# Where a row block of 640 keys is divided in the pass for row maxima and sums: 384 and 256 in place of 512 and 128

## The chip, the core and the metric

The kernel runs on one core of a Trainium2 chip. TensorE (PE in the rows) multiplies, VectorE (DVE), ScalarE (ACT) and GpSimd (POOL) do the elementwise work, and SyncE (SP) issues nearly all transfers. The metric is the device time of one execution in microseconds (us); lower is better.

## What is computed

One layer of a hybrid decoder on 1024 positions of 1024 channels: norm, one input projection, four head groups (A: sparse attention in three branches, B: differential attention, C: retention, D: a state space scan), gates, one output projection, residual, norm. The change touches only the softmax statistics of groups A and B. Cut to that:

```python
# group B, per head and map: all keys up to the query
s = einsum(q, k) * scale - slope * (t_q - t_k)
p = masked_softmax(s, t_q >= t_k)             # exp(s - max) / sum

# group A, branch "slc": as above (all 16 blocks of 64 keys are chosen)
# group A, branch "win": only the last 512 positions
p_w = masked_softmax(s_w, (dist >= 0) & (dist < WINDOW))
```

## The kernel before, in words

Positions are 8 blocks of 128, in two halves `u` of four blocks. Each attention head is worked twice. A **row pass** (`diff_rows` for group B, `nsa_rows` for A) has queries on partitions and only finds, for each query, the maximum and the sum of exponentials; `Stats.tile` does that for one tile of scores in PSUM. A second pass (`diff_out`, `nsa_out`) has keys on partitions, takes the shifts that the row pass left, and multiplies by the values into a bank `O`.

In the row pass a block `i` of 128 queries sees `n = (i + 1) * 128` keys, or at most 640 in the branch "win" (block `i` and the four before it). A bank of PSUM holds 512 float32 columns, so the keys are walked in pieces of 512. One piece is: matmul into a bank `S` (L173; in `nsa_rows` a second one at L1015 or L1026 for the low parts and positions), then `Stats.tile`: on VectorE the maximum (L466 without a mask, L468 with one), then on ScalarE the exponential with its sum (L469). The bank is free after that. There are three `S` banks, shared with the second pass. A matmul always takes at least 256 key columns, of which the statistics may use fewer, so that a last piece of 128 keys is multiplied as 256. A piece of at most 256 keys shares its bank: in `diff_rows` with the same piece of the other map, in `nsa_rows` (for `i % 4 < 2`) with the piece of the other branch.

A block of exactly 640 keys occurs in block 4 of both maps of four heads of group B, in block 4 of "slc" and in blocks 4 to 7 of "win" of four heads of group A: 28 blocks of 640 keys in all.

The order on each engine is made when the program is built: three streams (attention, recurrent groups, projections with the output at their end) are interleaved by weights, projection matmuls are kept behind a score matmul of some banks before, and a scheduler then orders the instructions of each engine by its own idea of their durations. So a change of one instruction's size can move others. GpSimd takes the low parts of weights (L248, L1182: raw minus high part) and parts of the second pass (L1083, L1085); SyncE's queue carries the loads and stores in order.

At the end `out_final` multiplies positions by the last two k tiles of the output weights (L1192 to L1194) into banks `mm` and `R`, and closes with the norm; the last steps of `nsa_out` (L1090) run among its first ones.

Of the kernel before, what the change touches and what calls it, by code (L numbers as in the profile page):

```python
# [20 lines left out]
S = 1024  # L21
D = 1024
# [32 lines left out]
def shape_constants():  # L55
    """Arrays that depend on the shapes alone: masks, decays, position rows."""
# [36 lines left out]
def merge(*streams):  # L93
    """Interleaves (generator, steps) streams in proportion to their steps; one that yields False waits for others."""
# [29 lines left out]
def hybrid_trunk_kernel(ctx: ExitStack, tc: tile.TileContext, a, out, dbg=None):  # L124
# [46 lines left out]
    def scores(tile_, *args, **kw):  # L171
        """A matmul into a bank of scores; the first of each bank paces the projections."""
        ins = T.matmul(tile_, *args, **kw)  # L173
        if kw["start"]:
            pace.append(ins)

    def paced(ins):
        """Keeps a projection's matmul behind the scores of a few banks before."""
        if len(pace) > AHEAD + FREE:
            tc.add_manual_dep(ins.ins, pace[-1 - AHEAD].ins.name, NOSYNC, reason="pace")  # L180

    def bc(ap, n):
        """[P, a] -> [P, a, n], each value repeated."""
        return ap[:, :, None].to_broadcast([ap.shape[0], ap.shape[1], n])

# [36 lines left out]
    def rsqrt_mean(dst, ssq, n):  # L222
        """dst = (ssq / n + eps) ** -0.5 on small tiles."""
# [10 lines left out]
    def weights(w, cols):  # L234
        """hi and lo parts of the columns `cols` = [(offset, width), ...] of w, by k tile."""
# [16 lines left out]
    def proj_t(cols, evac):  # L252
        """Columns on partitions, positions free: one bank per half of the positions."""
# [13 lines left out]
    def proj_n(cols, evac, w=None, step=True):  # L267
        """Positions on partitions, columns free: one bank per 128 positions."""
# [42 lines left out]
    def norm_x(ts):  # L311
        """Tiles of x: normalised, transposed, in hi and lo parts."""
# [97 lines left out]
    def evac_split(store, j, scale=1.0):  # L410
        """hi and lo parts of a tile of columns, kept in DRAM."""
# [21 lines left out]
    def ln_small(y, d, w):  # L433
        """y = ln(d) for d >= 1e-30, by one step from the exponent bits; w: scratch [4]."""
# [12 lines left out]
    class Stats:  # L447
        """Maxima and sums of the rows of `nb` score maps, half `u` of the positions: column (b, i, chunk)."""
# [12 lines left out]
        def tile(self, s, b, i, c, bound=None):  # L461
            """Largest score and sum of exponentials of one bank of scores; bound: NEG where masked, else 0."""
# [9 lines left out]
        def shifts(self, lng=None):  # L472
            """Columns -(max + ln(sum)) [+ ln(gate)], hi and lo: [(b, hi/lo, i)]."""
# [31 lines left out]
        def rows(self, d_sh):  # L505
            """The columns of shifts() to DRAM: [(b, hi/lo), S / 2]."""
# [6 lines left out]

    def diag_bound(w):
        return bounds[:, 640 - w:640]

    def pair(m):
        """A mask for both halves of a bank."""
# [13 lines left out]
    def diff_rows(h, u):  # L532
        """Row maxima and sums of both maps of a head, half u of the positions."""
# [5 lines left out]
        for i in range(HT * u, HT * u + HT):  # L539
            n = (i + 1) * P  # L540
            for c0 in range(0, n, 512):
                c1 = min(n, c0 + 512)
                if c1 - c0 <= 256:
# [4 lines left out]
                    for m in range(2):  # L548
                        st.tile(s[:, m, :c1 - c0], m, i, c0 // 512, diag_bound(c1 - c0))
                    yield  # L550
                    continue
                for m in range(2):
# [3 lines left out]
                    st.tile(s[:, :c1 - c0], m, i, c0 // 512, diag_bound(c1 - c0) if c1 == n else None)  # L556
# [9 lines left out]
    def score_t(s, w, parts, mask_lo, mask_hi):  # L566
        """Scores of a block of keys (partitions) against w positions."""
# [8 lines left out]
    def pv(o, e, vv, c0, w, first, last, hi_eng):  # L576
        """o[:, c0:c0 + w] += vv.T @ e, e in two parts."""
# [10 lines left out]
    def halves(dst, o):  # L588
        """dst = upper + lower half of o."""
# [3 lines left out]
    def wide(q, lo, hi):  # L593
        """Columns lo:hi of q, at least 256 of them, ending at hi."""
# [41 lines left out]
    # scratch in DRAM for group outputs in rows  # L636
# [3 lines left out]
    def diff_finish(j, u):  # L640
        """Root mean square of each head at each position."""
# [796 lines left out]
```

## Time and profile before

| what | value |
| --- | --- |
| timed runs | 774.78, 778.8, 780.49 us; median 778.8 |
| profiled execution | span 773.6 us (its time outside the span is not shown; the fastest timed run is 1.2 us above the span) |
| TensorE busy | 731.0 us, 95% of the span, 3876 matmuls |
| VectorE, ScalarE, GpSimd busy | 517.5 (67%), 414.4 (54%), 285.8 us (37%) |
| mean granted TensorE clock | 0.977 of full speed |

How to read the rows below: a timeline row gives the start, the duration, the engine, the line, the operation, what is written and read with its shape, and in brackets how long the engine was idle before it and for whom it waited. A TensorE row's duration includes its way through the array, so successive rows overlap; what a matmul costs in a dense stretch is the distance between starts. A matmul's shape gives partitions and moving columns. A row of a stretch ("windows") gives the busy time of each engine in a stretch, and behind it PEclk, the granted clock (1.00 is 2.4 GHz, 0.50 is 1.2 GHz).

### The profile page before, as it was taken

Reading aid. Unit: us, or ns where it says so; the run is one execution under the profiler, and the core shown is the slowest. Engines: PE = TensorE matmul, PEld = TensorE weight load, DVE = VectorE, ACT = ScalarE, POOL = GpSimd, SP = SyncE. Lnnn points to the kernel's source line nnn. Section 1 sums busy time; section 2 is a strip of 40 time slices with the busy share of each in tenths; the row PEclk is TensorE's granted clock in tenths of the full one; section 3 lists DMA queues with packets and bytes.
Section 4 is the critical chain, followed back from the end, with each engine's and each line's share of the span. In section 5 each row is a group of like instructions: output and inputs, shape, how many; then the busy total and the mean of one; then the engine's idle time right before and its main releaser. Section 6 shows DMA issues by size and latency. Waiting matters only on the chain.

```text
span 773.6 us, 12262 instructions
## 1 busy us (share of the span) xinstructions
PE 731.0 (95%) x3876; PEld 597.8 (77%) x3876; DVE 517.5 (67%) x1452; ACT 414.4 (54%) x1029; POOL 285.8 (37%) x365
## 2 busy tenths in 40 slices
PE   4989999999999999998989999999989989999994
PEld 4978877767887897786789888788766777788873
DVE  3852566545885855885787867667589897346476
ACT  5721565456667665762555554444456653453355
POOL 4221227111131114432422464554549742352336
PEclk9999999999999999999989999999998999999998
DMA  8548727647623623362222633335374224234365
GB/s 276 166 143 240 204 99 190 215 142 190 164 70 102 157 63 93 106 186 87 92 69 80 150 88 110 83 100 129 87 197 138 74 68 153 82 131 143 110 231 217
DMA packets 100844, 104.90 MB, mean 136 GB/s; under 512 B 15235, under 2 KB 76237, under 8 KB 100765
## 3 DMA queue, kind: packets, MB, share of 16 engines
q1 hardware_dynamic: 100684, 103.77, 45.0%
q8 instruction: 30, 0.49, 0.3%
q0 software_dynamic: 96, 0.36, 0.1%
q14 instruction: 34, 0.27, 0.1%
HBM read 71.91 MB, written 32.54 MB: 135 GB/s over the span
## 4 chain that ended last, share of the span: by engine, by line
PE 75%; DVE 11%; DMA 4%; issue 4%; POOL 2%; ACT 1%; SPq 1%; POOLq 0%; DVEq 0%; ACTq 0%
PE mm L260 10%; PE mm L259 10%; PE mm L261 10%; PE S L173 8%; PE O L1090 4%; PE mm L276 2%; PE mm L277 2%; PE mm L275 2%; DMA t<-d_cs 2%; PE S L1071 2%; PE R L1193 2%; PE R L1192 2%; PE mm L1192 2%; PE R L1194 2%; PE mm L1194 2%
## 5 line engine op out<-in xcount | busy, mean ns | idle before, releaser
L259 PE MATMUL mm<-h,whi 128*128 128x512 f32 x400 | 162.0, 405 | 2.2 <-DVE cwh L669 1.8
L260 PE MATMUL mm<-h,wlo 128*128 128x512 f32 x400 | 160.5, 401 | 0.0
L261 PE MATMUL mm<-h,whi 128*128 128x512 f32 x400 | 160.4, 401 | 0.0
L469 ACT ACTIVATE S<-S,sj 128x512 f32<-128x512 f32 (+3 forms) x192 | 103.4, 538 | 84.3 <-DVE sj L468 57.5
L173 PE MATMUL S<-b,b 100*128 100x256 f32 (+5 forms) x384 | 131.2, 367 | 5.3 <-ACT S L469 2.6
L248 POOL TENSOR_TENSOR wlo<-wraw,whi 128x1024 fp32r<-128x1024 f32 x29 | 69.3, 2391 | 177.4 <-ACT whi L247 158.0
L468 DVE CUSTOM_DVE_ANT_0 S<-S,mk 128x512 f32<-128x512 f32 (+3 forms) x144 | 70.5, 496 | 37.1 <-PE S L173 14.9
L259 PEld LDWEIGHTS mm<-h,whi 128*128 128x128 f32 x400 | 76.0, 190 | 18.0 <-issue 2.7
L173 PEld LDWEIGHTS S<-b,b 100*128 100x128 f32 (+1 forms) x384 | 72.5, 193 | 20.4 <-issue 5.0
L261 PEld LDWEIGHTS mm<-h,whi 128*128 128x128 f32 x400 | 75.9, 190 | 15.5
L260 PEld LDWEIGHTS mm<-h,wlo 128*128 128x128 f32 x400 | 75.9, 190 | 14.5 <-issue 0.4
L1085 POOL TENSOR_SCALAR pth<-e 128x512 fp32r<-128x512 f32 (+2 forms) x64 | 40.9, 644 | 61.9 <-ACT e L1080 40.4
L275 PE MATMUL mm<-whi,h 128*128 128x256 f32 (+1 forms) x192 | 57.7, 301 | 0.6 <-DVE ssmb L671 0.6
L1080 ACT ACTIVATE e<-S 128x512 f32<-128x512 f32 (+2 forms) x76 | 40.4, 543 | 31.4 <-PE S L1075 17.5
L276 PE MATMUL mm<-wlo,h 128*128 128x256 f32 (+1 forms) x192 | 57.3, 299 | 0.0
L277 PE MATMUL mm<-whi,h 128*128 128x256 f32 (+1 forms) x192 | 56.0, 297 | 0.0
L1086 DVE TENSOR_TENSOR ptl<-e,pth 128x512 fp32r<-128x512 f32 (+2 forms) x64 | 43.7, 694 | 17.1 <-POOL pth L1085 12.8
L623 ACT ACTIVATE e<-S 128x512 f32<-128x512 f32 (+1 forms) x64 | 35.8, 566 | 11.9 <-PE S L173 8.8
L466 DVE TENSOR_REDUCE sj<-S 128x1 f32<-128x512 f32 x48 | 32.7, 687 | 13.1 <-PE S L173 9.2
L275 PEld LDWEIGHTS mm<-whi,h 128*128 128x128 f32 x192 | 38.6, 201 | 1.5 <-ACT h L332 0.8
L247 ACT ACTIVATE whi<-wraw 128x1024 fp32r<-128x1024 f32 x29 | 30.6, 1056 | 17.1 <-DMA wraw<-in_w_in_dram 15.9
L625 DVE SCALAR_TENSOR_TENSOR e<-e,lam,e 128x512 f32<-128x512 f32 (+1 forms) x32 | 26.3, 821 | 19.9 <-ACT e L623 19.8
(326 smaller groups left out, 1723.4 us busy)
## 6 DMA issues: line engine op xcount, KB each, us to landing
wraw<-in_w_in_dram SPq DMA_DIRECT2D x27, 512.0 KB
b<-in_x_dram SPq DMA_DIRECT2D x8, 512.0 KB
t<-d_cs SPq DMA_DIRECT2D x32, 128.0 KB
wraw<-in_w_out_dram SPq DMA_DIRECT2D x16, 256.0 KB
ev<-in_x_dram SPq DMA_DIRECT2D x16, 256.0 KB
d_part<-ev SPq DMA_DIRECT2D x16, 256.0 KB
b<-d_part SPq DMA_DIRECT2D x8, 512.0 KB
out_dram<-b SPq DMA_DIRECT2D x16, 256.0 KB
```

Of the source, the lines that this page charges most:

```text
L173: ins = T.matmul(tile_, *args, **kw)
L248: G.tensor_tensor(lo, raw, hi.bitcast(F32), op=ALU.subtract)
L259: paced(T.matmul(p, w[k][0], h_hi[k][:, hs], start=(k == 0), stop=False))
L260: T.matmul(p, w[k][1], h_hi[k][:, hs], start=False, stop=False)
L261: T.matmul(p, w[k][0], h_lo[k][:, hs], start=False, stop=(k == NK - 1))
L275: paced(T.matmul(p, h_hi[k][:, hs], w[k][0], start=(k == 0), stop=False))
L276: T.matmul(p, h_hi[k][:, hs], w[k][1], start=False, stop=False)
L277: T.matmul(p, h_lo[k][:, hs], w[k][0], start=False, stop=(k == NK - 1))
L468: V.tensor_tensor_reduce(s, s, bound, -1.0, -NEG, ALU.add, ALU.min, nm)
L469: A.activation(s, s, AF.Exp, bias=nm, scale=1.0 if bound is None else -1.0, accum_out=self.d[:, b, i, c:c + 1])
L1085: G.tensor_scalar(hl[0], e, 1.0, 1.0, op0=ALU.mult, op1=ALU.mult)
L1086: V.tensor_tensor(hl[1], e, hl[0].bitcast(F32), op=ALU.subtract)
```

## The change

A helper `chunks(n)` cuts at 384 where `n` is 640 and at 512 otherwise, and returns the piece's number, which replaces `c0 // 512` as the column of the statistics. Both row passes walk its pieces. The mask of the window's lower edge is cut to the piece's width. Comments are removed as well. Behind line 514 lines move down by 4, behind `nsa_rows` by 3.

```diff
+    def chunks(n):
+        cut = 384 if n == 640 else 512
+        return [(j, c, min(n, c + cut) if j == 0 else n) for j, c in enumerate(range(0, n, cut))]
...
-            for c0 in range(0, n, 512):
-                c1 = min(n, c0 + 512)
+            for j, c0, c1 in chunks(n):
                 if c1 - c0 <= 256:
...
-                        st.tile(s[:, m, :c1 - c0], m, i, c0 // 512, diag_bound(c1 - c0))
+                        st.tile(s[:, m, :c1 - c0], m, i, j, diag_bound(c1 - c0))
...
-                    st.tile(s[:, :c1 - c0], m, i, c0 // 512, diag_bound(c1 - c0) if c1 == n else None)
+                    st.tile(s[:, :c1 - c0], m, i, j, diag_bound(c1 - c0) if c1 == n else None)
...
-                for c0 in range(0, n, 512):
+                for j, c0, c1 in chunks(n):
                     if i % HT < 2 and n - c0 <= 256:
-                        small.append((bi, b, b0, n, c0))
+                        small.append((bi, b, b0, n, c0, j))
                         continue
-                    c1 = min(n, c0 + 512)
...
-                    bound = diag_bound(c1 - c0) if diag else b_lower if lower else None
-                    st.tile(s[:, c0 - x0:c1 - x0], bi, i, c0 // 512, bound)
+                    bound = diag_bound(c1 - c0) if diag else b_lower[:, :c1 - c0] if lower else None
+                    st.tile(s[:, c0 - x0:c1 - x0], bi, i, j, bound)
...
-                for bi, b, b0, n, c0 in small:
-                    st.tile(s[:, bi - 1, xs[bi - 1]:w], bi, i, c0 // 512, diag_bound(w - xs[bi - 1]))
+                for bi, b, b0, n, c0, c in small:
+                    st.tile(s[:, bi - 1, xs[bi - 1]:w], bi, i, c, diag_bound(w - xs[bi - 1]))
```

What the edit does to the matmuls is seen in the first 640-key block of the program, head 0 of group B, on TensorE (`S` are banks of scores, `mm` a projection's bank). Before:

```order
L261 MATMUL mm_1092<-h_165,whi_1032 128x512
L173 MATMUL S_1059<-b_844,b_843 128x512
L173 MATMUL S_1069<-b_854,b_853 128x512
L173 MATMUL S_1085<-b_844,b_843 128x256
L173 MATMUL S_1085<-b_854,b_853 128x256
```

and with the change:

```order
L261 MATMUL mm_1092<-h_165,whi_1032 128x512
L173 MATMUL S_1059<-b_844,b_843 128x384
L173 MATMUL S_1069<-b_854,b_853 128x384
L173 MATMUL S_1085<-b_844,b_843 128x256
L173 MATMUL S_1085<-b_854,b_853 128x256
```

Nothing moved here; two matmuls of 512 columns became 384, and the shared bank's two stay 256 wide. In the whole program 28 matmuls at L173 and 20 at L1015 change so.

From the third head or so on, the scheduler's order differs in places. On TensorE, in the second pass of a head of group A (`O_6478` is its output bank, `ptl` and `pth` the low and high parts of exponentials; the `ptl` row is the one before which TensorE waits at 576.80 us in the trace), before:

```order
L1090 MATMUL O_6478<-pth_6503,b_3822 128x512
L776 MATMUL R_6380<-t_6367,t_6365 128x128
L778 MATMUL R_6380<-t_6367,t_6370 128x64 x2
L1090 MATMUL O_6478<-ptl_6504,b_3822 128x512
L820 MATMUL R_6432<-tri,ch_6428 128x128
```

and with the change:

```order
L1093 MATMUL O_6478<-pth_6503,b_3822 128x512
L173 MATMUL S_6565<-b_4989,b_3810 128x384
L1074 MATMUL S_6565<-b_4990,b_3811 128x384
L1078 LDWEIGHTS ident_bf
L1078 MATMUL S_6565<-mk,ident_bf 128x128
L173 MATMUL S_6577<-b_3810,b_6151 128x256
L1029 MATMUL S_6577<-b_3811,b_6152 128x256
L173 MATMUL S_6577<-b_3816,b_6151 128x256
L1029 MATMUL S_6577<-b_3817,b_6152 128x256
L173 MATMUL S_6586<-b_4989,b_3816 128x512
L1074 MATMUL S_6586<-b_4990,b_3817 128x512
L173 MATMUL S_6630<-b_3810,b_6151 128x384
```

Score matmuls that stood behind the `ptl` row now stand ahead of it, and the three of `R_6380` that stood between have gone further up.

The third place is the end of the last head's second pass on TensorE (`O_8021`), among the first products of the output (`R_8274`). Before:

```order
L1090 MATMUL O_8021<-ptl_8140,b_3824 128x384
L1090 MATMUL O_8021<-pth_8151,b_3822 128x384
L1090 MATMUL O_8021<-ptl_8152,b_3822 128x384
L1090 MATMUL O_8021<-pth_8165,b_3824 128x128
L1090 MATMUL O_8021<-ptl_8166,b_3824 128x128
```

and with the change:

```order
L1093 MATMUL O_8021<-ptl_8140,b_3824 128x384
L1093 MATMUL O_8021<-pth_8151,b_3822 128x384
L1196 MATMUL R_8274<-b_8229,h_7048 128x512
L1197 MATMUL R_8274<-b_8228,h_7049 128x512
L1195 MATMUL R_8274<-b_8228,h_7050 128x512
L1196 MATMUL R_8274<-b_8229,h_7050 128x512
L1197 MATMUL R_8274<-b_8228,h_7051 128x512
L1093 MATMUL O_8021<-ptl_8152,b_3822 128x384
L1093 MATMUL O_8021<-pth_8165,b_3824 128x128
L1093 MATMUL O_8021<-ptl_8166,b_3824 128x128
```

Five products of the output, which before stood ahead of this stretch, now stand inside it.

## Rows read from the trace of the kernel before

**Rows 1.** The page: TensorE's busy time, and granted clock in 40 slices.
```profile
PE 731.0 (95%) x3876; PEld 597.8 (77%) x3876; DVE 517.5 (67%) x1452; ACT 414.4 (54%) x1029; POOL 285.8 (37%) x365
PEclk9999999999999999999989999999998999999998
```

**Rows 2.** The page: the chain that ended last, by engine.
```profile
PE 75%; DVE 11%; DMA 4%; issue 4%; POOL 2%; ACT 1%; SPq 1%; POOLq 0%; DVEq 0%; ACTq 0%
```

**Rows 3.** Timeline of TensorE, dense stretch of 512-column matmuls: first and tenth.
```profile
150.36 0.40 PE L260 MATMUL mm<-h,wlo 128*128 128x512 f32 x1
...
152.46 0.40 PE L259 MATMUL mm<-h,whi 128*128 128x512 f32 x1
```

**Rows 4.** Timeline of TensorE: three 384-column matmuls in a row, and their successor.
```profile
602.21 0.34 PE L1090 MATMUL O<-pth,b 128*128 128x384 f32 x1
...
602.74 0.27 PE L755 MATMUL R<-tri,ch 128*128 128x128 f32 x1
```

**Rows 5.** Groups by form: count, then busy us and mean ns, idle before.
```profile
L469 ACT ACTIVATE S<-S,sj 128x512 f32<-128x512 f32 x92 | 60.6, 659 | 42.5 <-DVE sj L468 18.4 <-DVE sj L466 13.7 <-DVE sj L492 4.5
...
L466 DVE TENSOR_REDUCE sj<-S 128x1 f32<-128x512 f32 x48 | 32.7, 687 | 13.1 <-PE S L173 9.2 <-PE S L1015 3.5
...
L468 DVE CUSTOM_DVE_ANT_0 S<-S,mk 128x512 f32<-128x512 f32 x44 | 30.5, 698 | 14.5 <-PE S L173 8.7 <-PE S L1015 5.5
...
L468 DVE CUSTOM_DVE_ANT_0 S<-S,mk 128x384 f32<-128x384 f32 x28 | 15.5, 565 | 10.3 <-PE S L173 5.5 <-PE S L1015 4.7
L469 ACT ACTIVATE S<-S,sj 128x384 f32<-128x384 f32 x28 | 15.4, 549 | 14.7 <-DVE sj L468 13.2 <-DVE yr L500 1.5
...
L469 ACT ACTIVATE S<-S,sj 128x128 f32<-128x128 f32 x44 | 14.8, 337 | 16.8 <-DVE sj L468 15.9 <-DVE sj L502 0.3 <-DVE sm L224 0.3
...
L468 DVE CUSTOM_DVE_ANT_0 S<-S,mk 128x128 f32<-128x128 f32 x44 | 12.9, 293 | 8.7 <-PE S L1015 3.6 <-PE S L1026 2.7 <-ACT S L469 2.0
...
L469 ACT ACTIVATE S<-S,sj 128x256 f32<-128x256 f32 x28 | 12.5, 448 | 10.4 <-DVE sj L468 10.0 <-DVE sj L494 0.2
...
L468 DVE CUSTOM_DVE_ANT_0 S<-S,mk 128x256 f32<-128x256 f32 x28 | 12.1, 431 | 3.6 <-ACT S L469 2.1 <-PE S L173 0.5 <-PE S L1026 0.3
```

**Rows 6.** Timeline of VectorE: a maximum over 256 columns of a score bank.
```profile
387.34 0.41 DVE L990 TENSOR_REDUCE sj<-S 128x4 f32<-128x256 f32 x1
```

**Rows 7.** Timeline of TensorE at the end of the last second pass.
```profile
741.50 0.34 PE L1090 MATMUL O<-pth,b 128*128 128x384 f32 x1
...
742.06 0.45 PE L1090 MATMUL O<-ptl,b 128*128 128x384 f32 x1 [0.22 <-POOL ptl L1083]
...
743.76 0.33 PE L1090 MATMUL O<-ptl,b 128*128 128x128 f32 x1 [0.79 <-DVE ptl L1086]
```

**Rows 8.** Windows: stretch, its length, busy time by engine, granted clock, transfers.
```profile
577.70:587.80 10.10, 9.33 (x28) 6.63 (x28) 8.92 (x28) 7.79 (x26) 9.16 (x11) 0.50 0.76 254
632.30:635.60 3.30, 3.30 (x12) 2.70 (x12) 2.73 (x11) 2.43 (x7) 0.00 (x0) 0.50 0.00 1
744.90:748.20 3.30, 3.30 (x13) 2.82 (x12) 2.70 (x5) 1.93 (x5) 0.00 (x0) 0.50 0.96 355
```

**Rows 9.** Timeline of TensorE: three places where it sat idle about 2 us.
```profile
354.98 0.38 PE L586 MATMUL O<-ptl,b 128*128 128x256 f32 x1 [2.14 <-DVE ptl L584]
...
576.80 0.49 PE L1090 MATMUL O<-ptl,b 128*128 128x512 f32 x1 [1.96 <-DVE ptl L1086]
...
631.31 0.50 PE L173 MATMUL S<-b,b 128*128 128x512 f32 x1 [2.22 <-ACT S L469]
```

**Rows 10.** Waits of TensorE: for whom, us in total, times, longest.
```profile
PE S L173 <- ACT S L469: 2.6, 2, 2.2
```

**Rows 11.** Timeline: a small VectorE operation alone, and beside a GpSimd subtraction.
```profile
389.02 0.15 DVE L444 TENSOR_TENSOR sj<-sj 128x12 f32<-128x12 f32 x1
...
627.36 2.52 POOL L1122 TENSOR_TENSOR h<-ev,h 128x512 fp32r<-128x512 f32 x2
...
627.48 1.20 DVE L444 TENSOR_TENSOR sj<-sj 128x12 f32<-128x12 f32 x1
```

More of the change, by code (lines that the diff above doesn't have):

```diff
@@ L1020, in nsa_rows @@
                 s, xs = ps("S", [P, 2, 256]), [0, 0]
-                for bi, b, b0, n, c0 in small:
+                for bi, b, b0, n, c0, _ in small:
                     j = bi - 1
@@ L1027, in nsa_rows @@
                     xs[j], w = c0 - x0, n - x0
-                for bi, b, b0, n, c0 in small:
-                    st.tile(s[:, bi - 1, xs[bi - 1]:w], bi, i, c0 // 512, diag_bound(w - xs[bi - 1]))
+                for bi, b, b0, n, c0, c in small:
+                    st.tile(s[:, bi - 1, xs[bi - 1]:w], bi, i, c, diag_bound(w - xs[bi - 1]))
                 yield
```

## The prediction, made before the changed kernel was run

> **What bounds the kernel now.** First I read the page's busy times and clock: TensorE is busy 95% of the span, no other engine over 67%, and its granted clock is 2.4 GHz in nearly all slices [rows 1]. Then the chain of waits: 75% of what ended last is TensorE itself, 11% VectorE [rows 2]. So the end is set by how fast TensorE gets through its matmuls, and by the few places where it stands still. For the first I read the distance between starts in dense stretches of TensorE's timeline, since a row's own duration includes the way through the array: nine steps of 512 columns take 152.46 - 150.36 = 2.10 us, 0.233 us each [rows 3], and three of 384 columns 602.74 - 602.21 = 0.53 us, 0.177 us each [rows 4]. For the second I read the idle times in brackets: about 2 us at 354.98, 576.80 and 631.31 us [rows 9], and a chain of shorter ones at 742 to 744 us [rows 7]. Behind such a place the granted clock is 0.50, that is 1.2 GHz: 10.1 us long behind the one at 576.80, 3.3 us behind those at 631.31 and at 743.76 [rows 8]. At half speed with the engine busy nearly throughout, half of such a stretch is lost: about 5.0, 1.6 and 1.6 us. So one stall of 2 us costs 3.9 us at 631.31 (2.2 + 1.6, rounded) and 7.0 at 576.80 (1.96 + 5.0).
>
> **The edit itself, TensorE.** There are 28 blocks of 640 keys: 8 in group B (four heads, two maps) and 20 in group A (four heads, four blocks of "win" and one of "slc"). Each had a first piece of 512 and a last one of 128 keys, multiplied as 256. Now the pieces are 384 and 256, and the second matmul keeps its 256 columns. A block of B has one matmul per piece, one of A two: 8 + 2 x 20 = 48 matmuls go from 512 to 384 columns. By the steps above each saves 0.233 - 0.177 = 0.057 us, in all **2.7 us**. None of it is hidden behind other work where TensorE runs dense, which is nearly everywhere; no matmul, weight load or bank is added. What of it may be lost is where TensorE waits for a bank afterwards anyway.
>
> Per column the two widths cost the same, 0.456 and 0.460 ns [rows 3, 4]. [...]
>
> **VectorE and ScalarE.** The number of instructions stays, their widths change. With a mask (the 16 blocks of "win") the maxima took 698 + 293 = 991 ns and will take 565 + 431 = 996 [rows 5]. Without one (12 blocks) they took 687 + 293 = 980; a maximum over 384 columns without a mask is in no row, but lies between 0.41 us for 256 [rows 6] and 0.687 for 512 [rows 5]. I take the middle, 0.549, since the masked ones at 384 also lie in the middle of theirs, so 980 again; the ends are 841 and 1118, which over 12 blocks is -1.7 to +1.7 us on an engine with a third of its time free. The exponentials took 659 + 337 = 996 ns and will take 549 + 448 = 997 [rows 5]. So I cost both engines at nothing; the cover is their idle time, and if it were gone the 28 blocks would cost 16 x 0.005 + 28 x 0.001 = 0.1 us.
>
> **How long banks are held.** The first piece's bank comes free 133 + 110 = 0.24 us earlier. A bank shared by two last pieces is held for two maxima and an exponential more: 2 x 138 + 111 = 0.39 us longer. There are eight of these (four heads of B, block 4 of four heads of A). Another twelve banks hold one such piece and are held 138 + 111 = 0.25 us longer (blocks 5 to 7 of "win"). Over all banks that is 28 x -0.24 + 8 x 0.39 + 12 x 0.25 = -0.6 us: even. In the whole trace TensorE waits for a score bank behind the row pass's exponential twice, 2.6 us [rows 10], so I count nothing; if every one of the eight held TensorE up, it would be +3.1 us.
>
> **The order.** The scheduler's order shifts from about the third head on. I look only at places where TensorE stood still. At the end of the last second pass, from 741.50 to 743.76 us, it issued three matmuls in 2.26 us [rows 7]; at 0.177 each or less they needed at most 0.53, so 1.7 us were lost to the chain of parts from GpSimd and VectorE, and then 1.6 to the clock [rows 8]. In the new order five 512-column products, 5 x 0.233 = 1.2 us, stand between `pth_8151` and `ptl_8152`, just where the first wait was. They were done before this stretch, so they are not extra work but cover. The remaining pieces after `ptl_8152` are as bare as before, so the gain lies between 0 and 3.3 us; I take the middle, **1.7 us**. At 576.80 the new order puts nine score matmuls and more ahead of the waiting one, but also takes others away; there VectorE's and GpSimd's own order changed too, and I count nothing, with -7.0 as the far end. SyncE's queue holds the same transfers, a few some places later; no wait in [rows 9] is on a transfer, and I count nothing.
>
> **Sum.** -2.7 - 1.7 = -4.4 us. The profiled execution has a span of 773.6 us, 1.2 under the fastest run and 5.2 under the median of 778.8; it belongs to the fast end. By it the changed kernel's span would be 769.2; against the median, **774.4 us**.
>
> **The rivals.**
> *The gain is larger: more stalls go.* For it: at 354.98, 576.80 and 631.31 the order around the waiting matmul changed. Prices: 2.1 + 1.6 = 3.7 (the clock's share taken as at 631.31), 7.0 and 3.9, together 14.6. If half goes, 774.4 - 7.3 = 767.1. Against it: a new order makes new places as easily.
> *Slower: a new order starves TensorE at new places.* The mechanism is a small VectorE operation caught beside a GpSimd subtraction: 1.20 us at 627.48, while L1122 runs from 627.36, against 0.15 us for the same line at 389.02 [rows 11]. The next score bank's maximum then waits in VectorE's queue, and TensorE for the bank; this is what precedes the stall at 631.31. The place would be the row passes of the later heads, beside the weight subtractions. One such stall costs 3.9 us. Two of them would still end within 1%; from three more than before it decides: 778.8 - 2.7 + 3 x 3.9 = 787.8. Against it: all of the old stalls would have to stay.
> The Trainium skill, "SBUF — State Buffer", section "Who interferes with whom", has a rule for this: VectorE and GpSimd share a port pair that one instruction holds to its end, and the other blocks fully. Those rows agree with it.
> *The columns do not reach the end.* TensorE saves them but waits for the same banks a little later, and the shared banks add up to 3.1: 778.8 to 781.9. For it: 25% of the chain is not TensorE [rows 2]. Against it: the dense stretches. That the edit does not take effect can be left out: the built order has 384 in all 48.
>
> **How the numbers follow.** Chances: forecast 0.48, larger gain 0.24, starved 0.14, nothing reached 0.14. About 1%, 7.8 us, can be told from no change. Faster by over 1% means under 771.0: most of the second case and a little of the first, 0.25. Slower means over 786.6: nearly all of the starved case, 0.13. The rest, 0.62, is within 1%. The forecast's own range is 770.5 (the whole tail and a fast run) to 778.8. The range of 8 in 10 takes in most of the larger gain and the lighter stalls: 765 to 785.
>
> **What would show it.** The steps: 48 more matmuls of 384 columns at steps of 0.177 us, with busy TensorE down by about 2.7; VectorE and ScalarE busy within 2 us of 517.5 and 414.4; no idle over 0.5 us between `pth_8151` and `ptl_8152` near the end, and no stretch at 0.50 right behind it. Wrong would be: the number of stretches at 0.50 changing by two or more either way, or TensorE waiting for score banks far more than 2.6 us.

## The result, and the profile after

| | before | after |
| --- | --- | --- |
| median, beside each other on one chip (4 runs each) | 779.64 us (774.78 to 781.61) | 788.59 us (787.06 to 791.27) |
| profiled execution, span | 773.6 us | 786.3 us |

The ratio is 1.0109, with a 95% interval of 1.0069 to 1.0149: the change makes the kernel about 1% slower. The prediction, 774.4 us and faster, has the wrong sign, and the time lies outside its range.

First the page of the changed kernel: busy times, granted clock, and the chain that ended last.

```profile
PE 731.1 (93%) x3876; PEld 596.6 (76%) x3876; DVE 524.7 (67%) x1452; ACT 414.4 (53%) x1029; POOL 282.7 (36%) x365
PEclk9999999999999999999999899999977999999998
PE 63%; DMA 14%; DVE 12%; ACT 3%; POOL 3%; issue 3%; SPq 2%; DVEq 0%; POOLq 0%; ACTq 0%
```

TensorE's rows add up to what they did before [rows 1], in a span that is 12.7 us longer (the medians differ by 9.0; the profiled execution of before belongs to the fast end of its runs). So the difference is time without any work on TensorE; what more half clock adds to its busy time, the saved columns roughly take away. The chain says beside what: transfers have 14% of it where they had 4% [rows 2].

Did the columns come out as costed? TensorE's timeline in a dense stretch (start, duration, line, what it writes and reads), and then groups by form:

```profile
489.55 0.34 PE L173 MATMUL S<-b,b 128*128 128x384 f32 x1
489.72 0.34 PE L1018 MATMUL S<-b,b 72*128 72x384 f32 x1
489.90 0.34 PE L173 MATMUL S<-b,b 128*128 128x384 f32 x1
490.07 0.34 PE L1074 MATMUL S<-b,b 72*128 72x384 f32 x1
490.25 0.23 PE L1078 MATMUL S<-mk,ident_bf 128*128 128x128 bf16 x1
```
```profile
L469 ACT ACTIVATE S<-S,sj 128x384 f32<-128x384 f32 x56 | 31.0, 553 | 26.3 <-DVE sj L468 18.1 <-DVE sj L466 2.5 <-DVE sj L443 2.4
L468 DVE CUSTOM_DVE_ANT_0 S<-S,mk 128x384 f32<-128x384 f32 x44 | 24.6, 563 | 15.1 <-PE S L1018 9.7 <-PE S L173 5.4
L466 DVE TENSOR_REDUCE sj<-S 128x1 f32<-128x384 f32 x12 | 6.6, 552 | 1.7 <-PE S L173 1.5
```

Four matmuls of 384 columns take 490.25 - 489.55 = 0.70 us, 0.175 each, as in [rows 4]. The maximum without a mask takes 552 ns; the guess was 549. The edit does what the diff says, at the prices taken for one instruction.

Where did the time go? The group of the first projection matmul shows it in one line (busy, mean ns, then the idle time just before, and behind whom). Before, it has 2.2 us, 1.8 of them behind one wait (on `cwh`) at 50 us. Before, and then after:

```profile
L259 PE MATMUL mm<-h,whi 128*128 128x512 f32 x400 | 162.0, 405 | 2.2 <-DVE cwh L669 1.8 <-ACT ev L284 0.4
...
L259 PE MATMUL mm<-h,whi 128*128 128x512 f32 x400 | 162.5, 406 | 6.8 <-DVE ev L1132 4.6 <-DVE cwh L673 1.8 <-ACT ev L284 0.4
```

One stall of 4.6 us is new. Its place in the timelines of TensorE, VectorE, ScalarE, GpSimd and SyncE's queue:

```profile
441.59 0.40 PE L259 MATMUL mm<-h,whi 128*128 128x512 f32 x1
446.55 0.79 PE L259 MATMUL mm<-h,whi 128*128 128x512 f32 x1 [4.56 <-DVE ev L1132]
...
442.19 2.41 DVE L774 SCALAR_TENSOR_TENSOR t<-t,ncs,t 128x128 f32<-128x128 f32 x1 [2.13 <-POOL t L771]
445.49 0.34 DVE L774 SCALAR_TENSOR_TENSOR t<-t,ncs,t 128x128 f32<-128x128 f32 x1
446.09 0.40 DVE L1132 SCALAR_TENSOR_TENSOR ev<-ev,mm 128x256 f32<-128x256 f32 x1
...
439.79 0.37 ACT L1131 ACTIVATE ev<-mm 128x256 f32<-128x256 f32 x1
...
441.48 0.67 POOL L771 TENSOR_TENSOR t<-t,mk 128x256 f32<-128x256 f32 x1 [2.90 <-DMA t<-d_cs]
442.11 2.34 POOL L248 TENSOR_TENSOR wlo<-wraw,whi 128x1024 fp32r<-128x1024 f32 x1
...
435.86 0.32 SPq L769 DMA_DIRECT2D t<-d_cs  x1
436.50 0.93 SPq L856 DMA_DIRECT2D d_ret<-u  x1
437.52 0.38 SPq L770 DMA_DIRECT2D t<-d_cs  x1
```

Read it from below. SyncE issues the second load of `d_cs` at 437.52, behind a store. GpSimd's L771 waits for it until 441.48, VectorE's L774 for L771, and L774 then takes 2.41 us beside GpSimd's L248, which runs from 442.11 to 444.45 (the same L774 takes 0.58 us where L248 does not run beside it, in the third kernel of "The place at 446" below). Only after that does VectorE come to L1132, which empties the projection bank that TensorE wants. L1132 waits for none of this: its input from ScalarE's L1131 is there at 440.16. It stands behind L774 in the queue, in these places of VectorE's order (number, line, operation, what is written and read):

```
823 L774 SCALAR_TENSOR_TENSOR t_5040<-t_5040,ncs,t_5041 128x128
824 L1035 TENSOR_TENSOR ce_4268<-ce_4268,sj_4227 128x2x2x64
825 L500 CAST yr<-sj_4227 128x12
826 L774 SCALAR_TENSOR_TENSOR t_5040<-t_5040,ncs,t_5041 128x128
827 L994 TENSOR_REDUCE sj_5085<-S_5116 128x4
828 L1132 SCALAR_TENSOR_TENSOR ev_4750<-ev_4750,mm_4715 128x256
```

In the order of before the same eviction has number 803 and the two instructions on `t_5040` number 825: it stood 22 places ahead of them, and stands five behind. On GpSimd L248 moved from five places ahead of the addition L771 to one behind it.

The wait for the load is not new, only what stands behind it. Before (where the eviction is L1129 and the addition L767), GpSimd stands 3.53 us for the same load, and VectorE waits for GpSimd there too, but the eviction was done 7 us earlier, and between 440.5 and 446 us TensorE has no idle row:

```profile
437.11 0.40 DVE L1129 SCALAR_TENSOR_TENSOR ev<-ev,mm 128x256 f32<-128x256 f32 x1
...
444.65 0.67 POOL L767 TENSOR_TENSOR t<-t,mk 128x256 f32<-128x256 f32 x1 [3.53 <-DMA t<-d_cs]
```

What the stall cost, in windows (length, busy time by engine, granted clock, transfers), to be read like [rows 8]:

```profile
446.60:451.20 4.60, 4.60 (x11) 3.63 (x12) 1.96 (x10) 1.51 (x7) 0.00 (x0) 0.50 0.53 142
451.40:456.00 4.60, 4.60 (x30) 4.13 (x29) 2.71 (x10) 2.56 (x5) 3.14 (x4) 1.00 0.19 48
```

4.56 us idle, then 4.6 us at 1.2 GHz, of which half is lost: 6.9 us in one place. The second new place is a stretch at half clock from 581 to 601 us, twice as long as in [rows 8]; the third is the end of the last second pass, where [rows 7] was:

```profile
581.10:601.40 20.30, 16.23 (x49) 12.23 (x50) 19.20 (x54) 10.36 (x31) 12.72 (x18) 0.50 0.56 166
755.20:758.40 3.20, 3.20 (x10) 2.72 (x11) 2.60 (x6) 1.96 (x6) 0.52 (x1) 0.50 0.98 399
```
```profile
753.67 0.33 PE L1093 MATMUL O<-ptl,b 128*128 128x128 f32 x1 [3.02 <-DVE ptl L1089]
...
752.32 0.69 DVE L1123 SCALAR_TENSOR_TENSOR ev<-b,ev 128x512 f32<-128x512 f32 x1 [5.16 <-DMA ev<-d_z]
752.93 0.69 DVE L1089 TENSOR_TENSOR ptl<-e,pth 128x512 fp32r<-128x512 f32 x1
```

There the order does the same: L1123 waits 5.16 us for a load, and the part `ptl` that TensorE wants stands behind it.

### The profile page after: what moved, and what is told of

The parts are those of the page before. It is cut to its first block, busy times and chain, and to the rows that moved or that the text cites. A ratio compares the mean times of both kernels' runs of the same rounds, so it can differ in the third digit from the quotient of the medians.

```text
span 786.3 us, 12264 instructions
## 1 busy us (share of the span) xinstructions
PE 731.1 (93%) x3876; PEld 596.6 (76%) x3876; DVE 524.7 (67%) x1452; ACT 414.4 (53%) x1029; POOL 282.7 (36%) x365
## 4 chain that ended last, share of the span: by engine, by line
PE 63%; DMA 14%; DVE 12%; ACT 3%; POOL 3%; issue 3%; SPq 2%; DVEq 0%; POOLq 0%; ACTq 0%
PE mm L259 9%; PE mm L260 8%; PE mm L261 8%; PE S L173 6%; DMA t<-d_cs 4%; PE O L1093 3%; PE mm L275 2%; PE mm L277 2%; PE mm L276 2%; DMA b<-d_dk 2%; PE S L1074 2%; PE R L1195 2%; DMA b<-in_w_in_dram 1%; PE R L1196 1%; PE R L1197 1%
## 5 line engine op out<-in xcount | busy, mean ns | idle before, releaser
L259 PE MATMUL mm<-h,whi 128*128 128x512 f32 x400 | 162.5, 406 | 6.8 <-DVE ev L1132 4.6
L469 ACT ACTIVATE S<-S,sj 128x384 f32<-128x384 f32 (+3 forms) x192 | 103.6, 540 | 71.7 <-DVE sj L468 43.7
L173 PE MATMUL S<-b,b 100*128 100x256 f32 (+5 forms) x384 | 131.6, 366 | 8.7 <-ACT e L1083 3.3
L248 POOL TENSOR_TENSOR wlo<-wraw,whi 128x1024 fp32r<-128x1024 f32 x29 | 69.3, 2389 | 182.6 <-ACT whi L247 167.5
L468 DVE CUSTOM_DVE_ANT_0 S<-S,mk 128x384 f32<-128x384 f32 (+3 forms) x144 | 71.9, 507 | 35.9 <-PE S L173 15.4
L259 PEld LDWEIGHTS mm<-h,whi 128*128 128x128 f32 x400 | 76.3, 191 | 23.4 <-DVE ev L1132 5.0
L173 PEld LDWEIGHTS S<-b,b 100*128 100x128 f32 (+1 forms) x384 | 72.9, 194 | 23.7 <-ACT e L1083 4.3
L1088 POOL TENSOR_SCALAR pth<-e 128x512 fp32r<-128x512 f32 (+2 forms) x64 | 39.1, 615 | 57.0 <-ACT e L1083 29.7
L774 DVE SCALAR_TENSOR_TENSOR t<-t,ncs,t 128x128 f32<-128x128 f32 x32 | 20.4, 676 | 33.9 <-POOL t L771 33.1
L466 DVE TENSOR_REDUCE sj<-S 128x1 f32<-128x512 f32 (+1 forms) x48 | 31.0, 652 | 17.1 <-PE S L173 12.1
```

Source lines behind the costliest of these rows:

```text
L248: G.tensor_tensor(lo, raw, hi.bitcast(F32), op=ALU.subtract)
L259: paced(T.matmul(p, w[k][0], h_hi[k][:, hs], start=(k == 0), stop=False))
L468: V.tensor_tensor_reduce(s, s, bound, -1.0, -NEG, ALU.add, ALU.min, nm)
L469: A.activation(s, s, AF.Exp, bias=nm, scale=1.0 if bound is None else -1.0, accum_out=self.d[:, b, i, c:c + 1])
```

## The experiments

The theory after reading both traces (T1): the sizes are worth what was costed, and the loss is the **new order** that the scheduler made from the new sizes. Rivals: the sizes themselves (T2), and that any new order scatters the time by about 1% (T3).

Sizes and order can be taken apart, since both programs have the same instructions under the same names. A kernel below that is said to have an order of another program has that order fixed on all five engines by edges that only order and wait for nothing:

```diff
+    traced = {i.name: i for i in nc.cur_bb.bb.instructions}
+    for seq in PIN:                      # one list of names per engine
+        names = ["I-%d" % n for n in seq if "I-%d" % n in traced]
+        for first, then in zip(names, names[1:]):
+            tc.add_manual_dep(traced[then], first, NOSYNC, reason="pin")
```

All ratios are to the kernel before, run beside on the same chip.

### Sizes and order apart

The first has the sizes 384 and 256, the second 512 and 128, each with the other program's order.

> The change's sizes (384 and 256 in place of 512 and 128), with the order of every engine held to that of the kernel before. If the order is the cause (T1): only the columns are left, 48 x 0.057 = 2.7 us faster, so 776 to 777 us where before is 779.6, and the waits of VectorE for loads of t and ev stand as in before (POOL t for d_cs about 58 us, none of 5 us at ev). If the sizes themselves are the cause (T2: banks held longer, larger evictions at bad places): 787 to 789 us. If any rebuild scatters (T3): no forecast, within 770 to 790.

> The sizes of before (512 and 128), with the order of every engine held to that of the changed kernel. T1 (order): slower than the changed kernel by the columns, 788.6 + 2.7 = about 791 us, with the same late loads (t at 578, ev at 752). T2 (sizes): as before, about 779 us. T3: no forecast.

Measured: new sizes in the old order 779.54 us, ratio 0.9987 (0.9962 to 1.0013). Old sizes in the new order 790.99 us, ratio 1.0144 (1.0115 to 1.0173). T2 falls: without the new order the new sizes cost nothing, and without the new sizes the new order costs all of it and more. By the second against the change, 1.0144 - 1.0109, the sizes are worth 0.35%, 2.7 us, give or take 3.9 (95%, as everywhere below); by the first 0.13%, 1.0 us, give or take 2.0. Both fit the 2.7 us forecast, and both fit nothing. The first kernel has its order fixed by the same edges and loses nothing, so the edges are not what costs. The group of L259 goes with the order, not with the sizes. The page's busy times and that group, in the old order with new sizes, and then in the new order with old sizes (its lines have the numbers of before):

```profile
PE 730.5 (94%) x3876; PEld 597.9 (77%) x3876; DVE 517.6 (67%) x1452; ACT 413.5 (53%) x1029; POOL 287.8 (37%) x365
...
L259 PE MATMUL mm<-h,whi 128*128 128x512 f32 x400 | 162.1, 405 | 2.2 <-DVE cwh L673 1.8
```
```profile
PE 736.9 (93%) x3876; PEld 598.6 (76%) x3876; DVE 522.2 (66%) x1452; ACT 414.0 (52%) x1029; POOL 283.7 (36%) x365
...
L259 PE MATMUL mm<-h,whi 128*128 128x512 f32 x400 | 162.7, 407 | 7.6 <-DVE ev L1129 5.4
```

### Does any new order cost this much?

Three programs whose order the scheduler made anew: the cut in one row pass only, in the other only, and the kernel before with one weight of the interleaving changed.

```diff
 against the changed kernel
-    def chunks(n):
-        cut = 384 if n == 640 else 512
+    def chunks(n, cut=512):
+        cut = cut if n == 640 else 512
...
-            for j, c0, c1 in chunks(n):
+            for j, c0, c1 in chunks(n, 384):     # in diff_rows (first), in nsa_rows (second)
```
```diff
 against the kernel before
-W_ATT, W_REC, W_PROJ = 400, 70, 660
+W_ATT, W_REC, W_PROJ = 400, 70, 661
```

> The new cut in diff_rows alone (8 of the 48 matmuls of 512 columns become 384: 0.5 us fewer columns), the order left to the scheduler, which makes another one. T2 (the sizes cost it, in proportion to the places): about 780 to 781. T1 and T3 (any new order draws new places at which queues block): anything from 775 to 792, not in proportion to the number of matmuls.

> The new cut in nsa_rows alone (40 of the 48 matmuls, 2.2 us fewer columns), the order left to the scheduler. T2: 40 of 48 parts of the change's loss, about 787. T1 and T3: 775 to 792, not in proportion.

> The kernel before with all its sizes; only the projections' share in the interleaving is 661 in place of 660 (W_PROJ), so the scheduler makes another order of the same instructions. T3: an order that differs by chance is as likely to cost as the change's, 784 to 792. If the kernel before is an order like any other: 775 to 784. T2 says 779, since no size changes.

Measured: `diff_rows` alone 782.82 us, 1.0022 (1.0001 to 1.0043); `nsa_rows` alone 790.77, 1.0133 (1.0103 to 1.0164); the weight alone 778.74, 0.9979 (0.9958 to 1.0001). So a new order does not cost 1% as such, and T3 in that form falls: of four orders that the scheduler made, two are within 0.25% of the old one and two are 1.1% and 1.3% slower. Both slow ones have the cut in `nsa_rows`. That fits a proportion to the number of shortened matmuls too, which was T2's forecast here; but with the order held the sizes cost nothing, and the stalls are not at the same places: with `nsa_rows` alone none is at 446.

### Where in the order

Four kernels with the new sizes, in which a stretch has the changed kernel's order and the rest that of before (the edit in words; the lists are long).

```diff
-PIN = order of one program
+PIN = order of program X up to what it has done at time T, then what is left in the order of program Y
```

> The change's sizes; every engine follows the changed kernel's order up to what that kernel has done at 566 us, and from there the order of before for all that is left. If the loss sits where the traces put it (T1), the time that TensorE has lost beyond its columns is 4.8 us more than with the old order when the new order reaches 566 us: 779.5 + 4.8 = about 784. If one place decides for all: 788.6 or 779.5. T2: 788.6.

> The change's sizes; the order of before up to 566 us, then the changed kernel's order up to what it has done at 708 us, then the order of before. T1: the stretch with 20.5 us at half clock costs what the traces show between these places, 2.4 us net: about 782; if the half clock there comes whole with the order (10.2 us more at half speed): 784.6. T2: 788.6.

> The change's sizes; the order of before up to 700 us, then the changed kernel's order to the end. There the last partial sum is stored at 746 us where the order of before stores it at 732, and the loads of it start at 748 where before starts them at 740. T1: 779.5 + 3.7 us = about 783. If the tail's stall only follows from delays ahead of it: 779.5. T2: 788.6.

> The change's sizes; the changed kernel's order up to 425 us, ahead of the stall of 4.56 us at 446.55, and the order of before for the rest. T1: of the 4.8 us that the new order costs up to 566 us, the first 425 us have about 1.5, the stall at 446 the others: 781. T2: 788.6.

| new order in | median us | ratio | above the old order (0.9987) |
| --- | --- | --- | --- |
| up to 566 us | 785.32 | 1.0070 (1.0039 to 1.0100) | 0.83%, 6.5 us |
| 566 to 708 us | 782.83 | 1.0035 (1.0012 to 1.0058) | 0.48%, 3.7 us |
| from 700 us | 780.90 | 1.0011 (0.9980 to 1.0042) | 0.24%, 1.9 us |
| up to 425 us | 779.20 | 0.9978 (0.9950 to 1.0005) | none |

The three parts add up to 12.1 us where the whole is 1.0109 - 0.9987, 9.5 us; each has an uncertainty of some 2 to 3 us, so they add up within it. All of the first part lies between 425 and 566 us, and the group of L259 has 5.3 us behind L1132 in the first kernel of the table, none in the last. The tail alone can't be told from nothing.

### The place at 446

The first two kernels have the changed kernel's order, in which only VectorE's queue is edited; the third also GpSimd's.

```diff
 VectorE, near 752 us (both of the first two kernels)
-  L1123 ev, L1089 ptl, L1125 h, L1089 ptl
+  L1089 ptl, L1089 ptl, L1123 ev, L1125 h
 VectorE, near 442 and near 579 us (the second kernel)
-  L774 t, L774 t, ..., L1132 ev       and   L774 t, L774 t, ..., L286 ptl
+  L1132 ev, L774 t, L774 t            and   L286 ptl, L774 t, L774 t
```
```diff
 the third kernel: VectorE and GpSimd near 440 us, nothing else
-  L774 t, ..., L774 t, L994, L1132 ev       GpSimd: L771 t, L248 wlo
+  L1132 ev, L774 t, ..., L774 t, L994       GpSimd: L248 wlo, L771 t
```

> The changed kernel with its own order, but on VectorE two instructions of the late row pass (L1123 on ev and L1125 on h) are put behind the two evictions of ptl (L1089) that TensorE waits for. T1: TensorE's 3.02 and 0.65 us of idle time at 753.67 and 755.06 go, and with them the 3.4 us at half clock (1.7 us): 788.6 - 5.4 at the most, about 784; where the clock drops elsewhere all the same, 785.5. T2 and T3: 788.6, since no size changes.

> As the kernel with the tail moved, and at two more places the two VectorE instructions on t (L774) that wait for a late load of d_cs are put behind the next eviction that TensorE waits for (near 442 and near 579 us). T1: beside the tail's 3 to 5 us also 4.6 us of idle time and up to 3.4 us of half clock at 446, and of the 20.5 us at half clock from 581 up to 10 us: 772 to 778. T2: 788.6. If the late loads only move the wait on to whoever reads t next: 780 to 785.

> The changed kernel with its own order but for two moves near 440 us: on VectorE the eviction L1132 goes ahead of L774, which waits for a load of d_cs; on GpSimd the L771 that waits for that load goes behind L248. If the eviction's place behind the load is the cause of the stall at 446.55: 4.56 us of idle time and up to 3.4 us for 6.8 us at half clock go, 781 to 784 us where the changed kernel is 788.6. If the wait only moves on to the next reader of d_cs: 786 to 789.

Measured: tail moved 789.37 us, 1.0125 (1.0102 to 1.0147), no gain; three places moved 785.77, 1.0074 (1.0038 to 1.0111), less than expected. In the tail the wait went over to the next reader of a load: TensorE now stands 3.26 us at 756.96, behind L1253, which stands behind L1123 and L1125 and itself waits 0.42 us for the load of its partial sums. At 446 it went over to GpSimd, whose L248 stands behind the waiting L771:

```profile
443.97 0.80 PE L260 MATMUL mm<-h,wlo 128*128 128x512 f32 x1 [3.03 <-POOL wlo L248]
...
440.95 0.67 POOL L771 TENSOR_TENSOR t<-t,mk 128x256 f32<-128x256 f32 x1 [3.66 <-DMA t<-d_cs]
441.57 2.34 POOL L248 TENSOR_TENSOR wlo<-wraw,whi 128x1024 fp32r<-128x1024 f32 x1
```

With VectorE's queue alone freed the wait stays; GpSimd's alone was not tried. With both moves, 783.46 us, ratio 1.0032 (1.0010 to 1.0053): 0.77%, 6.0 us, less than the changed kernel, give or take 3.5. Its rows there:

```profile
441.51 0.42 DVE L1132 SCALAR_TENSOR_TENSOR ev<-ev,mm 128x256 f32<-128x256 f32 x1
442.15 0.58 DVE L774 SCALAR_TENSOR_TENSOR t<-t,ncs,t 128x128 f32<-128x128 f32 x1 [0.21 <-POOL t L771]
...
438.30 2.38 POOL L248 TENSOR_TENSOR wlo<-wraw,whi 128x1024 fp32r<-128x1024 f32 x1
441.44 0.67 POOL L771 TENSOR_TENSOR t<-t,mk 128x256 f32<-128x256 f32 x1 [0.77 <-PE R L837]
```

L774 takes 0.58 us, L771 waits for TensorE and no longer for the load, and TensorE has no idle row behind L1132. Last, the same two moves in the kernel that has the new order up to 566 us and the old one from there:

> The change's sizes; the changed kernel's order up to 566 us with the two moves near 440 us, from there the order of before. If the stall at 446 is all that the new order loses up to there: 785.3 - 6 = 779 us, as with the old order throughout. If the new order has other losses there: 782 to 785.

Measured: 777.85 us, 0.9981 (0.9956 to 1.0005), where it was 785.32, 1.0070, without them. **All that the new order loses up to 566 us is this one place**: 0.89%, 6.9 us, by the runs, give or take 3.0, and 6.9 us by the rows.

### The place from 566 us

Here the loads looked like the cause. GpSimd's timeline and a window of the changed kernel: L771 waits 6.69 us for `d_cs`, while the transfer engines are busy 0.98 of the time and TensorE 2.79 us of 5:

```profile
578.40 0.67 POOL L771 TENSOR_TENSOR t<-t,mk 128x256 f32<-128x256 f32 x1 [6.69 <-DMA t<-d_cs]
...
575.00:580.00 5.00, 2.79 (x19) 2.29 (x17) 1.58 (x5) 1.45 (x4) 1.60 (x2) 1.00 0.98 264
```

All three kernels have the changed kernel's order with moves on SyncE's queue; the second and third also have those of the place at 446.

```diff
 SyncE, near 570 us (first two kernels; the third has only the move of h)
-  d_z store, ev, t<-d_cs, t<-d_cs, ev, d_ssm store, h, h, ev, h<-d_ret, ch<-d_conv, d_z store, ch, ch
+  t<-d_cs, t<-d_cs, d_z store, ev, ev, d_ssm store, ev, h<-d_ret, ch<-d_conv, h, h, ch, ch, d_z store
```

> The changed kernel with its own order but for SyncE's queue near 570 us: two loads of d_cs (L769, L770) go ahead of a store of d_z that they stood behind (2.4 us of waiting), the large loads of h (L1139, L1140, 512 KB each) go behind L756, and a load of ch (L818, L819) goes ahead of the next store of d_z. If the loads' place is the cause: TensorE's stalls of 2.21, 1.36 and 2.60 us at 579.64, 581.57 and 586.89 go, and of 20.5 us at half clock about 10, so up to 11 us; with half of it given back 780 to 785. If the transfers are late for another reason, or another wait stands behind: 786 to 790.

> The moves near 440 us and near 570 us together, nothing else. If the two places carry the loss of the new order (7.2 and 3.7 us by the kernels that had one stretch of it): 776 to 780, no slower than before. If other places of the order come up once these are free: 781 to 786.

> The changed kernel's order with the two moves near 440 us, and of the moves near 570 us one alone: the two loads of h (L1139, L1140, 512 KB each) go behind L756 on SyncE's queue, so that they are not in flight with the loads of d_cs. If these loads delay d_cs: its flight of 6.1 us falls to some 4 and TensorE waits 2 us less near 575, with a shorter stretch at half clock: 783.5 - 3 to - 6 = 777 to 780. If not: 783 to 784; if h is then late for its readers: 785 to 788.

Measured: 794.47 us, 1.0176 (1.0145 to 1.0206), worse than the change; with the place at 446 freed 786.71, 1.0059 (1.0036 to 1.0082); only `h` later 782.10, 1.0021 (0.9994 to 1.0048), not to be told from 1.0032. In the first, the load of `ev` behind the store of `d_z` came late instead: SyncE's queue held it back for 4.3 us until the store had landed, and VectorE then stood 4.58 us for it (SyncE's wait, VectorE's row):

```profile
SPq L1122 <- DMA d_z<-ev: 4.3, 1, 4.3
...
581.72 0.75 DVE L1123 SCALAR_TENSOR_TENSOR ev<-b,wret,ev 128x512 f32<-128x512 f32 x1 [4.58 <-DMA ev<-d_z]
```

In the last the load of `d_cs` is in time (GpSimd waits for TensorE instead), and the time stays:

```profile
574.95 0.67 POOL L771 TENSOR_TENSOR t<-t,mk 128x256 f32<-128x256 f32 x1 [5.65 <-PE R L841]
```

So the late load of `d_cs` is not shown to cost this stretch: with it in time, against the third kernel of "The place at 446", TensorE's wait at this place falls from 2.59 us to 1.36, and the time by 0.11%, 0.9 us, give or take 2.7. In the kernel with the new order from 566 to 708 us alone, TensorE's largest stall there is beside a VectorE that waits for yet another load:

```profile
578.00 0.58 PE L1055 MATMUL O<-pth,vvc 128*128 128x256 f32 x1 [4.99 <-DMA h<-d_ssm]
...
576.20 0.75 DVE L1123 SCALAR_TENSOR_TENSOR ev<-b,wret,ev 128x512 f32<-128x512 f32 x1 [5.19 <-DMA ev<-d_z]
```

The first row names a load of `h`, which L1055 does not read, so what released it is not shown. That the order costs some 3.7 us here, give or take 2.7, is measured; which instruction or transfer does it stays open.

### A version that beats both?

The new sizes in the old order, with six moves at places where TensorE stood behind a queue (the ones at 355, 388, 548, 578, 606 and 633 us), and then with three loads of `h` put later on SyncE's queue:

```diff
 VectorE   + L588 ptl ahead of L774, L774;  L994, L995, L997 ahead of L441;  L1089 ptl ahead of L1035, L497;  L468 ahead of L443
 GpSimd    + L1088 pth ahead of L771;  L1086 ptl ahead of L771
 SyncE     + L1139, L1140, L1166 behind L818, L819, L769, L770      (second kernel only)
```

> The change's sizes with the order of before, and six moves in it, each where the trace of that kernel (new sizes, old order; 779.5 us) shows TensorE idle for 1 to 2.2 us behind an instruction that its own data did not hold up: on VectorE one ptl (L588, 354.5 us) goes ahead of the two L774 that wait for GpSimd, the row maxima L994, L995, L997 (388.5) ahead of a small L441 that stood 2.27 us beside GpSimd's L248, one ptl (L1089, 577.8) ahead of L1035 and L497, the second L468 of a bank (633.1) ahead of L444 and L445; on GpSimd one pth (547.5) and one ptl (605.7) ahead of an L771 that waits for a load. If place in a queue is what costs (T1): about 10 us of idle time at the most and up to 10 us for stretches at half clock; with half of it given back elsewhere 769 to 774 us. If the idle time only moves on (T2, T3): 777 to 781.

> The change's sizes, the order of before with the six moves made already (778.3 us), and on SyncE three large loads of h (L1139, L1140, L1166, 512 KB each) put behind the loads of ch and d_cs that TensorE's work near 577 us needs. If the burst of loads is what makes the stall of 2.85 us at 582.03 there and the half clock after it: 770 to 775. If not: 778.

Measured: 778.25 us, 0.9975 (0.9947 to 1.0003), and 782.97, 1.0013 (0.9982 to 1.0045). A miss both times. The stalls at 355 and 578 went, the one at 633 stood again with 2.13 us, and new ones of 2.00 us at 360.39 and 2.85 us at 582.03 came; with the loads of `h` later the last was still there (2.86 us at 579.96), and one of 3.67 us followed. No version is faster than the kernel before by more than the runs can tell; the best medians of the new sizes are 777.85 to 779.5 us, all in an order without the place at 446.

## Why the prediction was wrong

**The columns: right in the price, not told from nothing in the sum.** At 384 columns the rows after show 0.175 us, 0.456 ns per column, as in [rows 3] at 512. -2.7 us was forecast in all; with the order held the runs give -2.7 (new order, interval -6.6 to +1.1) and -1.0 (old order, interval -3.0 to +1.0). TensorE's busy time, which was to fall by 2.7, went from 731.0 to 730.5 in the old order and from 736.9 to 731.1 in the new one, with different shares of half clock in it.

**VectorE, ScalarE, banks: right in what they cost.** ScalarE's busy time is 414.4 us both times. VectorE's rose by 7.2 us, more than the 2 us allowed, but not through the sizes: with them in the old order it is 517.6. Most of it is one group, that of the L774 above; before (L770), and then after:

```profile
L770 DVE SCALAR_TENSOR_TENSOR t<-t,ncs,t 128x128 f32<-128x128 f32 x32 | 13.9, 472 | 34.0 <-POOL t L767 32.7 <-DMA t<-d_cs 1.2
...
L774 DVE SCALAR_TENSOR_TENSOR t<-t,ncs,t 128x128 f32<-128x128 f32 x32 | 20.4, 676 | 33.9 <-POOL t L771 33.1 <-DMA t<-d_cs 0.8
```

It goes with the order: 13.7 us with the new sizes in the old order, 20.6 with the old sizes in the new. TensorE's own wait for L469 went from 2.6 us [rows 10] to 1.7.

**The order: this step failed.** It says: "I look only at places where TensorE stood still." An order is judged just as much at places where TensorE did not stand still before; between 440.5 and 446 us the kernel before has no idle row of TensorE, so nothing drew the eye there, and there the new order lost 6.9 us. The two orders side by side show the eviction move 27 places against the instructions on `t`, before anything is run. The step had the wrong sign: -1.7 us was taken, +11 is what the new order costs at the old sizes (1.0144). For 6.9 us of that the cause is shown; for the part from 566 us on, some 4 us, it stays open.

**SyncE's queue: looked at in the wrong rows.** "SyncE's queue holds the same transfers, a few some places later; no wait in [rows 9] is on a transfer, and I count nothing." Those rows are TensorE's. GpSimd waited for loads before as well, 3.53 us at 444.65, and VectorE's idle time in the two group rows above, nearly all of it behind GpSimd's addition, is 34.0 us before and 33.9 after. So what is new at 446 is not a later load: it was issued at 438.99 us before and at 437.52 after. A store now stands between the two loads of `d_cs` (the row L856), but the kernel with both moves leaves SyncE's queue as it is and has the time back. The step did not ask which eviction comes to stand behind such a wait.

**The tail: the first wait went, as forecast, and a larger one came two pieces later.** Between `pth_8151` and `ptl_8152`, where TensorE stood 0.22 us [rows 7], there is no idle row any more; but the step called the later pieces "as bare as before" and counted no loss for them, and the one that waited 0.79 us there now waits 3.02 us and has the half clock behind it. What the tail's order costs, 1.9 us, can't be told from nothing.

**The rival "starved".** Its time, 787.8, was close, in part by luck, and its chance of 0.14 too small. Its mechanism is a part only. L774's 2.41 us beside L248 are its collision, about 2 of the 4.56 us; the rest is the wait for a load, ahead of the eviction in the queue. And it asked for three more stalls at 3.9 us, where one of 6.9 and a longer stretch at half clock did it. The Trainium skill's "SBUF — State Buffer", section "Who interferes with whom", says that VectorE and GpSimd share a port pair, which the one that issues first holds for its whole instruction; this row agrees with it, L774 ending 0.15 us after L248. What the rival left out stands on another page of the Trainium skill, "PSUM — Partial Sum Buffer", section "Engine vs sequencer instructions": the queues of VectorE, ScalarE and GpSimd are strictly first in, first out. The trace agrees: L1132, with its input ready at 440.16 (ScalarE's L1131 ends), starts at 446.09.

**The rival "larger gain"** had a part of its mechanism come true: the stalls of 2.14 us at 354.98 and 2.22 us at 631.31 [rows 9] are gone, and so are the stretches at half clock behind them: after, the longest wait of the first kind is 1.1 us, of the second 0.6. So the new order both takes stalls away and makes new ones, and the loss is what is left over. "All of the old stalls would have to stay", said against "starved", was not needed.

**The rival that the columns do not reach the end** stays open: the runs fit 2.7 us and fit nothing.

**The signs of being wrong that were named** did not come up. TensorE waited less for score banks than before, and the stretches at 0.50 went from seven to six. Their length would have shown it: by the mean granted clock, 0.977 and 0.971, it is 2 x 0.023 x 773.6 = 36 us before and 2 x 0.029 x 786.3 = 46 after.

## What to carry to other kernels

Where a scheduler orders the work, an edit of sizes is two changes, and they can be timed apart: fix the order, change the sizes, and the reverse. Read the difference of the two orders for evictions that free TensorE's banks, and look whether an instruction that waits for a load (or for an engine that waits for one) has come to stand ahead of one on VectorE or GpSimd; price it as idle time plus half of the stretch at half clock that follows. Here, freeing VectorE's queue alone handed the wait on to GpSimd's, which stood behind the same load; with both freed the 6 us came back.

## What the hardware showed beside this

- A small VectorE instruction that started inside a GpSimd subtraction ended just behind it: L774 ran from 442.19 to 444.60 us beside L248 (442.11 to 444.45), 2.41 us, and took 0.58 us in the kernel where L248 was moved away.
- After 4.56 us without work TensorE ran at 1.2 GHz for the next 4.6 us although it was busy throughout, and at 2.4 GHz from 451.4 on.
- SyncE's queue stands still until a store has landed when the next load waits for that store: in the changed kernel the store of L1218 goes out at 746.12 and the load of L1122 at 748.17, 2.05 us later. In the first kernel of "The place from 566 us" it was 4.8 us (573.77 to 578.59); why it took longer there is not shown.
